# A hybrid decoder layer on one core: longer planned transfers into the row tiles, from the first superblock's end on

## Chip, cores, metric

The kernel runs on one core of one Trainium2 chip. The metric is device microseconds of one execution, as the median of several runs.

## The reference, cut to what matters

One layer of a decoder stack: a norm, one wide projection, three branches (an RWKV-7 recurrence, sliding-window attention with rotary angles and sinks, cross-attention into 256 memory tokens), a gated merge, an output projection and the residual.

```
h = rms_norm(x, norm_g[l])
p = h @ w_in[l]
(p_r, p_k, p_v, p_w, p_a, z_a, p_q, p_sk, p_sv, z_b, p_xq, z_c, p_gate) = jnp.split(p, split_points, axis=-1)
y_a = rwkv7_mix(p_r, p_k, p_v, p_w, p_a, ...) * jax.nn.silu(z_a)
y_b = sliding_window_sink_attn(p_q, p_sk, p_sv, positions, ...) * jax.nn.silu(z_b)
y_c = memory_cross_attn(p_xq, mem, ...) * jax.nn.silu(z_c)
gates = jax.nn.sigmoid(p_gate).reshape(bsz, t, N_BRANCHES, D_MODEL)
merged = (gates[:, :, 0] * (y_a @ w_proj_a[l]) + gates[:, :, 1] * (y_b @ w_proj_b[l])
          + gates[:, :, 2] * (y_c @ w_proj_c[l]))
x = x + merged @ w_out[l]
```

x has 2048 rows of 1024 float32 numbers; w_in is 1024 by 7552.

## The kernel before, in words

**Tiles.** The 2048 tokens are worked in four superblocks of 512. In a superblock, h of the norm lies as eight tiles of 128 channels by 512 tokens, each split into a high part (hH) and a low part (hL) in TensorE's float32r format. A projection (`proj`, `gemm3`, lines 534 to 536) multiplies 8 such tiles by a 128-channel block of w_in: three matmuls for each tile (high by high, low by high, high by low), 24 matmuls of 128x128 by 512, into one of two PSUM banks named mm. The weights are split too: ScalarE copies the high part (L515), VectorE takes the difference (L516). In the first superblock all weights come raw and are split, and most are then kept in DRAM as pairs (k) for the later ones, which load them ready.

**Streams.** Two generators are woven into one program for each superblock: `stream_r` (the recurrence: four prepared pairs of heads, an inversion, a chain of eight chunks) and `stream_f` (cross-attention, sliding window, merges of the branches b and c, and the gates of branch a, each a projection and a tanh, L1306). A third, `x_sums`, loads the next superblock's rows of x for the norm: eight tiles of 128 by 512, all named sx with one buffer, each loaded by ScalarE's queue (L1360) and squared and summed by ScalarE (L1362).

**The end of a superblock.** The merge of branch a (L1321 adds one to the gate and multiplies it with the sum in the mm bank, L1322 adds it to the accumulator mB), the split of the merged tiles (L1326 on ScalarE, L1328 on VectorE) and the output projection (L1338 to L1340, then L1345 adds x, loaded into ya tiles, and L1346 stores) run there. Between them stands the preparation of the next superblock: `rope_tables` loads the positions into an rt tile, computes angles on VectorE (L597 to L616) with two sines on ScalarE (L612, L614); `x_scales` makes the row scales (L1370, L572, L574, L1375); `x_cols` loads eight tiles of x columns into rt tiles by ScalarE's queue (L1384), scales them on VectorE (L1387) and splits them into hH (L1389, ScalarE) and hL (L1390, VectorE). The sine and the tanh of the gates lie in different function tables of ScalarE, and a load of a table (ACT_TABLE_LOAD) stands wherever the order goes from one to the other.

**The planner.** The program order of each engine is not the order of the code. `steps` makes a `Step` of each instruction with its dependences, a rank (its place in the code, moved for some kinds) and costs by the functions `cost_PE`, `cost_ACT` and so on. `lay_out` is a list scheduler: it plays the program forward with these costs, and each engine takes, of the steps that it believes ready at that moment, the one with the lowest rank. `order` then fixes that order on each engine. A DMA costs its queue 420 ns and ends 2200 ns after its issue (4200 for tiles parked in DRAM), not before the wires are free, plus its bytes over 380 a nanosecond. On top comes `late`, which is 5000 for the sx tiles and 0 for all others:

```
if s.bytes:
    wires = s.end = max(wires, s.end) + s.bytes / 380
    s.end += s.late
```

The planner only sets the order. At run time an engine waits in that order for what an instruction really needs. A longer planned transfer makes the steps that read the tile look ready later, so that others are placed ahead of them; and as every later choice depends on the clock of the plan, the order of other engines can move as well.

Of the kernel before, what the change touches and what calls it, by code (L numbers as in the profile page):

```python
# [51 lines left out]

LAT = {"PE": 200, "DVE": 45, "ACT": 35, "POOL": 80, "SP": 30}
NAMES = {mybir.EngineType.PE: "PE", mybir.EngineType.DVE: "DVE", mybir.EngineType.Activation: "ACT",
         mybir.EngineType.Pool: "POOL", mybir.EngineType.SP: "SP"}
# [2 lines left out]
class Step:  # L60


    def __init__(self, ins, masks):
        self.ins, self.eng = ins, NAMES[ins.engine]
        self.reads, self.writes = ([self.region(a.bass_ap, masks) for a in aps if getattr(a, "bass_ap", None) is not None]
                                   for aps in (ins.ins, ins.outs))
        self.reads, self.writes = ([r for r in l if r] for l in (self.reads, self.writes))
        self.before, self.after, self.opens, self.group, self.end, self.next = set(), [], [], [], None, None
        self.lat = LAT[self.eng]
        self.chain = self.eng == "PE" and any(r[0].startswith(("Zt", "W_", "R_")) or r[0] in ("W", "R") for r in self.reads)  # L70
        if self.eng == "PE":
            self.lat = 600
        outs = [a.bass_ap for l in (ins.outs, ins.ins) for a in l if getattr(a, "bass_ap", None) is not None]
        rows = [a.offset // math.prod(list(a.tensor.shape)[1:]) for a in outs[:1] + [a.bass_ap for a in ins.ins if getattr(a, "bass_ap", None) is not None]]
        self.rows = rows[0], max(rows)
        self.bytes = 512 * self.n((self.writes + self.reads)[0]) if self.is_dma() else 0
        getattr(self, "cost_" + ("SP" if self.bytes else self.eng))()

    def is_dma(self):
# [62 lines left out]
    def cost_SP(self):  # L142
        parked = any(r[0].startswith(("fq", "fb", "fv", "fn", "fy")) for r in self.reads + self.writes)
        self.dur, self.busy = 4200 if parked else 2200, 420
        self.late = 5000 if any(r[0].startswith("sx") for r in self.writes) else 0


def steps(instructions, manual, groups, follow, ahead=1000):

    out, masks, seen, byname, opener = [], {}, {}, {}, {}  # L150
    for ins in instructions:
        if isinstance(ins, mybir.BassTilePoolBoundary):
            continue
        s = Step(ins, masks)
        for rs, w in ((s.reads, False), (s.writes, True)):
            for name, parts, words, _, psum, _ in rs:
                s.before |= {q for q, w2, p2, m2 in seen.get(name, ()) if (w or w2 or psum) and q is not s and p2 & parts and m2 & words}
        for name, parts, words, *_ in s.reads:
            seen.setdefault(name, []).append((s, False, parts, words))
        for name, parts, words, *_ in s.writes:  # L160
            old = seen.setdefault(name, [])
            old[:] = [x for x in old if x[0] is s or x[2] & ~parts or x[3] & ~words] + [(s, True, parts, words)]
        s.before |= {byname[x] for x in manual.get(ins.name, ())}
        s.before |= {opener.setdefault(r[0], s) for r in s.writes + s.reads} - {s}
        for b in s.before:
            b.after.append(s)
        byname[ins.name] = s
        s.rank = len(out)
        if any(r[0].startswith(("whl", "raw")) and (s.bytes or r[5] == F32R) for r in s.writes):
            s.rank = max(s.rank - ahead, min(s.rank, FRONT))  # L170
        if s.eng != "PE" and any(r[4] for r in s.reads):
            s.rank -= 600 + 1000 * any(r[0].startswith("mm_") for r in s.reads)
        if s.eng == "DVE" and s.writes and s.writes[0][0].startswith(("ibc", "Yi")):
            s.rank += 500
        out.append(s)
    for a, b in follow.items():
        byname[a].next = byname[b]
    for names in groups:
        group = [byname[n] for n in names]
        group[0].group = group[1:]  # L180
        needs = set().union(*(s.before for s in group)) - set(group)
        for s in group:
            for b in needs - s.before:
                b.after.append(s)
            s.before |= needs
    return out
# [123 lines left out]
def order(tc, manual, groups, follow):  # L310

    orders = lay_out(tc, steps(list(tc.nc.cur_bb.bb.instructions), manual, groups, follow))
    how = mybir.DependencyInfo(mybir.DependencyClass.NoSync, mybir.DependencyReason.DATA)
    for l in orders.values():
        for a, b in zip(l, l[1:]):
            tc.add_manual_dep(b.ins, a.ins.name, how, reason="order")
# [1237 lines left out]
```

## Time and profile before

| | |
|---|---|
| median of three runs | 2141.29 us (2141.21 to 2143.42) |
| the profiled execution | 2142.16 us, its span 2140.3 us |
| TensorE (PE) busy | 2124.0 us |
| its weight loads (PEld) | 1750.1 us |
| VectorE (DVE) | 1429.2 us |
| ScalarE (ACT) | 803.4 us |
| GpSimd (POOL) | 140.5 us |
| granted TensorE clock | 1.000 |

Matmuls are pipelined: a matmul of 512 columns is recorded with 394 ns, and the next one starts earlier than that. In rows of groups the number after the bar is the busy time, then the mean of one in ns, then the idle time of the engine ahead of them. In a timeline row the columns are start, duration, engine (a q behind it is its queue of instructions), line, operation, tiles, and in brackets the idle time of the engine just before and what ended it. In a row of waits stand what waited, at which line, for what, then the total, the number of times and the longest. The superblocks' output projections run at 528 to 572, 1051 to 1095, 1573 to 1616 and 2093 to 2136 us.

### The profile page before, as it was taken

Reading aid. Unit: us, or ns where it says so; the run is one execution under the profiler, and the core shown is the slowest. Engines: PE = TensorE matmul, PEld = TensorE weight load, DVE = VectorE, ACT = ScalarE, POOL = GpSimd, SP = SyncE. Lnnn points to the kernel's source line nnn. Section 1 sums busy time; section 2 is a strip of 40 time slices with the busy share of each in tenths; the row PEclk is TensorE's granted clock in tenths of the full one; section 3 lists DMA queues with packets and bytes.
Section 4 is the critical chain, followed back from the end, with each engine's and each line's share of the span. In section 5 each row is a group of like instructions: output and inputs, shape, how many; then the busy total and the mean of one; then the engine's idle time right before and its main releaser. Section 6 shows DMA issues by size and latency. Waiting matters only on the chain.

```text
span 2140.3 us, 37430 instructions
## 1 busy us (share of the span) xinstructions
PE 2124.0 (99%) x14248; PEld 1750.1 (82%) x14248; DVE 1429.2 (67%) x3246; ACT 803.4 (38%) x1699; POOL 140.5 (7%) x180
## 2 busy tenths in 40 slices
PE   9999999999999999999999999999999999999999
PEld 7888788778888888878788888887888888888787
DVE  7879888568477777546647778736455777873532
ACT  7655555335343343313424434410423334331220
POOL 1001000001001000001001000000100010000000
PEclk9999999999999999999999999999999999999999
DMA  9987898988876678695877667877676666768665
GB/s 333 361 284 266 275 300 273 348 297 263 277 213 200 189 218 233 199 313 189 278 255 216 199 178 229 235 235 256 214 265 215 210 196 203 230 188 273 209 207 180
DMA packets 308594, 519.17 MB, mean 243 GB/s; under 512 B 89280, under 2 KB 175552, under 8 KB 308416
## 3 DMA queue, kind: packets, MB, share of 16 engines
q1 hardware_dynamic: 292288, 487.42, 71.4%
q10 hardware_dynamic: 16128, 29.37, 4.2%
q8 instruction: 113, 1.85, 0.4%
q14 instruction: 65, 0.53, 0.1%
HBM read 378.80 MB, written 137.89 MB: 241 GB/s over the span
## 4 chain that ended last, share of the span: by engine, by line
PE 90%; DVE 4%; DMA 3%; issue 1%; ACT 1%; SPq 0%; POOL 0%; ACTq 0%; DVEq 0%
PE mm L535 22%; PE mm L534 22%; PE mm L536 22%; PE mm L1338 1%; PE mm L1340 1%; PE mm L1339 1%; PE rw L999 1%; PE rw L1016 1%; PE oo L1287 1%; PE rw L831 1%; DVE whl L516 1%; PE rw L850 1%; PE oo L831 1%; DMA raw<-in_w_in 1%; PE rw L921 0%
## 5 line engine op out<-in xcount | busy, mean ns | idle before, releaser
L534 PE MATMUL mm<-hH,whl 128*128 128x512 f32 x1888 | 743.6, 394 | 0.4 <-DVE carry L742 0.4
L535 PE MATMUL mm<-hL,whl 128*128 128x512 f32 x1888 | 743.7, 394 | 0.2 <-DVE hL L1390 0.2
L536 PE MATMUL mm<-hH,whl 128*128 128x512 f32 x1888 | 742.1, 393 | 0.0
L534 PEld LDWEIGHTS mm<-hH,whl 128*128 128x128 f32 x1888 | 354.8, 188 | 71.3 <-ACT big L851 0.7
L535 PEld LDWEIGHTS mm<-hL,whl 128*128 128x128 f32 x1888 | 354.9, 188 | 71.2 <-DVE hL L1390 0.6
L536 PEld LDWEIGHTS mm<-hH,whl 128*128 128x128 f32 x1888 | 354.8, 188 | 70.8
L515 ACT ACTIVATE whl<-raw 128x512 fp32r<-128x512 f32 x174 | 108.9, 628 | 124.8 <-PE mm L536 85.4
L516 DVE TENSOR_TENSOR whl<-raw,whl 128x512 fp32r<-128x512 f32 x174 | 119.9, 691 | 50.2 <-ACT whl L515 48.2
L534 PE MATMUL mm<-yh,whl 128*128 128x512 f32 x384 | 151.0, 393 | 0.1
L535 PE MATMUL mm<-yl,whl 128*128 128x512 f32 x384 | 150.2, 391 | 0.0
L536 PE MATMUL mm<-yh,whl 128*128 128x512 f32 x384 | 150.2, 391 | 0.0
L1306 ACT ACTIVATE gt<-mm 128x512 f32<-128x512 f32 x64 | 38.0, 593 | 216.7 <-PE mm L536 216.5
L534 PEld LDWEIGHTS mm<-yh,whl 128*128 128x128 f32 x384 | 72.1, 188 | 15.7 <-ACT gt L1306 0.5
L535 PEld LDWEIGHTS mm<-yl,whl 128*128 128x128 f32 x384 | 72.1, 188 | 14.9 <-DVE yl L1065 0.3
L536 PEld LDWEIGHTS mm<-yh,whl 128*128 128x128 f32 x384 | 72.1, 188 | 14.8
L1321 DVE SCALAR_TENSOR_TENSOR gt<-gt,mm 128x512 f32<-128x512 f32 x32 | 22.0, 687 | 92.3 <-PE mm L536 92.1
L487 POOL TENSOR_SCALAR st<-st 128x4 f32<-128x4 f32 (+1 forms) x32 | 12.5, 391 | 1004.9 <-DVE st L1219 407.4
L1345 DVE SCALAR_TENSOR_TENSOR ya<-mm,ya 128x512 f32<-128x512 f32 x16 | 11.0, 689 | 94.7 <-PE mm L1340 94.7
L1255 ACT ACTIVATE g<-g,mxs,st 128x128 f32<-128x128 f32 x128 | 61.6, 483 | 26.6 <-DVE mxs L1248 26.6
L892 DVE TENSOR_TENSOR ibc<-km,Yi 128x126 f32<-128x126 f32 (+22 forms) x248 | 62.8, 253 | 6.2 <-DMA km<-fn 0.6
L893 DVE TENSOR_TENSOR Yi<-Yi,ibc 128x126 f32<-128x126 f32 (+22 forms) x248 | 62.9, 254 | 5.5
L491 POOL TENSOR_TENSOR st<-st,mhalf 128x8 f32<-128x8 f32 (+1 forms) x36 | 56.2, 1562 | 3.0
(1807 smaller groups left out, 3586.0 us busy)
## 6 DMA issues: line engine op xcount, KB each, us to landing
whl<-k SPq DMA_DIRECT2D x474, 512.0 KB, 4.1
k<-whl SPq DMA_DIRECT2D x162, 512.0 KB, 4.7
raw<-in_w_in SPq DMA_DIRECT2D x118, 256.0 KB, 4.1
fq<-big SPq DMA_DIRECT2D x64, 256.0 KB, 4.5
fb<-big SPq DMA_DIRECT2D x64, 256.0 KB, 4.7
big<-fq SPq DMA_DIRECT2D x32, 512.0 KB, 6.4
big<-fb SPq DMA_DIRECT2D x32, 512.0 KB, 5.6
ya<-in_x ACTq DMA_DIRECT2D x32, 256.0 KB, 5.5
```

Source lines behind the costliest of these rows:

```text
L491: G.tensor_tensor(out, out, mhalf[:, :n], op=ALU.pow)
L515: S.activation(w[:, 0], raw, AF.Copy)
L516: V.tensor_tensor(w[:, 1], raw, w[:, 0].bitcast(F32), op=ALU.subtract)
L534: PE.matmul(out, lh, rh, start=i == 0, stop=False)
L535: PE.matmul(out, lh, rl, start=False, stop=False)
L536: newest[0] = PE.matmul(out, ll, rh, start=False, stop=i == n - 1).ins.name
L831: m = PE.matmul(g[:, c], BK[h, c0 + c], Q[h, c0 + c], start=True, stop=True)
L892: V.tensor_tensor(bc[:, :m, :w], Nb[:, s, s + 1:].unsqueeze(1).to_broadcast([128, m, w]), B[:, :m, s:s + 1].to_broadcast([128, m, w]), op= ...
L893: V.tensor_tensor(B[:, :m, s + 1:], B[:, :m, s + 1:], bc[:, :m, :w], op=ALU.add)
L1255: S.activation(P_, P_, AF.Exp, scale=r2[:, b, i:i + 1], bias=mx[:, b, i:i + 1], accum_out=mx[:, b, 2 + i:3 + i])
L1306: S.activation(t, gp, AF.Tanh, scale=0.5)
L1321: V.scalar_tensor_tensor(g, g, 1.0, pp, op0=ALU.add, op1=ALU.mult)
```

## The change

`late` is now taken from a small table by the name of the tile that a step writes, and is set to 0 for the first 3000 steps.

```
+LATE = {"sx": 5000, "rt": 3500, "xr": 6000}
...
+        self.late = next((t for n, t in LATE.items() for r in self.writes if r[0].startswith(n)), 0)
...
     def cost_SP(self):
         parked = any(r[0].startswith(("fq", "fb", "fv", "fn", "fy")) for r in self.reads + self.writes)
         self.dur, self.busy = 4200 if parked else 2200, 420
-        self.late = 5000 if any(r[0].startswith("sx") for r in self.writes) else 0
...
         s.rank = len(out)
+        if s.rank < 3000:
+            s.late = 0
```

Only DMAs use `late` in `lay_out`. So loads into rt tiles (the positions and the columns of x at the three boundaries) are planned 3500 ns longer. No DMA writes a tile whose name begins with xr (the rows of x for the output go to ya), so that entry names nothing. The bound of 3000 steps lies inside the first superblock: its first four sx loads come before it and are now planned 5000 ns shorter than before, the other four keep their 5000. The instructions themselves are the same, except for the table loads, which follow from the order.

In the order, TensorE's row differs between about 160 and 500 us of the old trace (the first superblock), and at three small places, one at each boundary. The other engines differ in the same stretches. The changed file is three lines longer, so that each line number there is three higher (L1387 becomes L1390).

VectorE at the second boundary. Before (g2 holds a gate, mm the bank with the projection of branch a, rt the columns of x):

```order
L1322 TENSOR_TENSOR mB_9089<-mB_9089,g2_11070 128x512
L1387 TENSOR_TENSOR rt_11382<-rt_11382,rt_11190 128x512
L1387 TENSOR_TENSOR rt_11387<-rt_11387,rt_11190 128x512
L1321 SCALAR_TENSOR_TENSOR g2_11101<-g2_11101,mm_11335 128x512
L1328 TENSOR_TENSOR mB_11331<-mB_9089,g2_11329 128x512
L516 TENSOR_TENSOR whl_11506<-raw_11507,whl_11506 128x512
L1322 TENSOR_TENSOR mB_9456<-mB_9456,g2_11101 128x512
L1321 SCALAR_TENSOR_TENSOR g2_11132<-g2_11132,mm_11361 128x512
```

And changed:

```order
L1325 TENSOR_TENSOR mB_9089<-mB_9089,g2_11070 128x512
L1331 TENSOR_TENSOR mB_11305<-mB_8938,g2_11303 128x512
L1331 TENSOR_TENSOR mB_11331<-mB_9089,g2_11329 128x512
L1324 SCALAR_TENSOR_TENSOR g2_11101<-g2_11101,mm_11335 128x512
L1325 TENSOR_TENSOR mB_9456<-mB_9456,g2_11101 128x512
L519 TENSOR_TENSOR whl_11506<-raw_11507,whl_11506 128x512
L1331 TENSOR_TENSOR mB_11352<-mB_9456,g2_11350 128x512
L1324 SCALAR_TENSOR_TENSOR g2_11132<-g2_11132,mm_11361 128x512
L1325 TENSOR_TENSOR mB_9556<-mB_9556,g2_11132 128x512
L1331 TENSOR_TENSOR mB_11378<-mB_9556,g2_11376 128x512
L1390 TENSOR_TENSOR rt_11382<-rt_11382,rt_11190 128x512
```

The first two scalings of columns (L1387) stood ahead of the last two products with a gate (L1321); now all products, sums and splits of the merge stand ahead of the first scaling.

ScalarE at the second boundary, some 25 us earlier. Before:

```order
L1306 ACTIVATE g2_11070<-mm_11041 128x512
L612 ACT_TABLE_LOAD
L612 ACTIVATE rt_11160<-rt_11155 128x512
L515 ACTIVATE whl_11260<-raw_11261 128x512
L614 ACTIVATE rt_11160<-rt_11155 128x512
L1362 ACTIVATE sx_11038,ss_6534<-sx_11038 128x512
L1306 ACT_TABLE_LOAD
L1306 ACTIVATE g2_11101<-mm_11072 128x512
L515 ACTIVATE whl_11307<-raw_11308 128x512
L1306 ACTIVATE g2_11132<-mm_11103 128x512
```

And changed:

```order
L1309 ACTIVATE g2_11070<-mm_11041 128x512
L518 ACTIVATE whl_11260<-raw_11261 128x512
L615 ACT_TABLE_LOAD
L615 ACTIVATE rt_11160<-rt_11155 128x512
L1309 ACT_TABLE_LOAD
L1309 ACTIVATE g2_11101<-mm_11072 128x512
L1365 ACTIVATE sx_11038,ss_6534<-sx_11038 128x512
L617 ACT_TABLE_LOAD
L617 ACTIVATE rt_11160<-rt_11155 128x512
L518 ACTIVATE whl_11307<-raw_11308 128x512
L1309 ACT_TABLE_LOAD
L1309 ACTIVATE g2_11132<-mm_11103 128x512
```

The tanh of a gate has come between the two sines, with a load of its table ahead of it and one of the sine's behind. The third boundary has the same pattern.

VectorE in the first superblock, about 263 us into the old trace, where L1275 cuts the probabilities of a head pair to its window (as_ is a PSUM bank with them) and L846 scales the keys of the recurrence. Before:

```order
L839 TENSOR_TENSOR big_2202<-yps_2652,gmask_179 64x512
L516 TENSOR_TENSOR whl_3320<-raw_3321,whl_3320 128x512
L1275 TENSOR_TENSOR g2_3121<-as__3114,over_181 64x256
L1275 TENSOR_TENSOR g2_3133<-as__3126,over_181 64x256
L821 SCALAR_TENSOR_TENSOR rr__2527<-rr__2527,dv_182,rk__2245 128x512
L516 TENSOR_TENSOR whl_3464<-raw_3465,whl_3464 128x512
L846 TENSOR_TENSOR big_2205<-big_2205,Pl_658 128x1024
```

And changed:

```order
L842 TENSOR_TENSOR big_2203<-oo_2653,gmask_179 64x512
L519 TENSOR_TENSOR whl_3320<-raw_3321,whl_3320 128x512
L1278 TENSOR_TENSOR g2_3121<-as__3114,over_181 64x256
L1278 TENSOR_TENSOR g2_3133<-as__3126,over_181 64x256
L1278 TENSOR_TENSOR g2_3121<-as__3114,over_181 64x256
L519 TENSOR_TENSOR whl_3464<-raw_3465,whl_3464 128x512
L1278 TENSOR_TENSOR g2_3133<-as__3126,over_181 64x256
L849 TENSOR_TENSOR big_2205<-big_2205,Pl_658 128x1024
```

All four cuts stand together now (two stood further ahead before), L821 and the first shift of the next keys (L740) have moved ahead of them, and L846 follows the last cut directly. On TensorE, 38 large matmuls instead of 24 stand between the products of the recurrence (L831) and the ones that need the cuts (L1287). On ScalarE in the same superblock the Square of the second sx tile stands ahead of L1170 and three rows behind its load, where it stood behind L1172 and six rows behind.

More of the change, by code (lines that the diff above doesn't have):

```diff
@@ L51 @@
 NPV = _n
+LATE = {"sx": 5000, "rt": 3500, "xr": 6000}
 LAT = {"PE": 200, "DVE": 45, "ACT": 35, "POOL": 80, "SP": 30}
@@ L76, in __init__ @@
         self.bytes = 512 * self.n((self.writes + self.reads)[0]) if self.is_dma() else 0
+        self.late = next((t for n, t in LATE.items() for r in self.writes if r[0].startswith(n)), 0)
         getattr(self, "cost_" + ("SP" if self.bytes else self.eng))()
@@ L144, in cost_SP @@
         self.dur, self.busy = 4200 if parked else 2200, 420
-        self.late = 5000 if any(r[0].startswith("sx") for r in self.writes) else 0
 def steps(instructions, manual, groups, follow, ahead=1000):
@@ L168, in steps @@
         s.rank = len(out)
+        if s.rank < 3000:
+            s.late = 0
         if any(r[0].startswith(("whl", "raw")) and (s.bytes or r[5] == F32R) for r in s.writes):
```

## The prediction

> **What bounds the kernel now.** I read the page first (busy shares, chain), then the waits of TensorE by stretch, then the timelines where they lie.
>
> ```profile
> PE 2124.0 (99%) x14248; PEld 1750.1 (82%) x14248; DVE 1429.2 (67%) x3246; ACT 803.4 (38%) x1699; POOL 140.5 (7%) x180
> PE 90%; DVE 4%; DMA 3%; issue 1%; ACT 1%; SPq 0%; POOL 0%; ACTq 0%; DVEq 0%
> ```
>
> TensorE is busy 99% of the span, and 90% of the chain that ended last is its own matmuls. The change takes no matmul away and only moves instructions, so it can win no more than the pauses of TensorE, and lose only what new pauses cost. The pauses lie in few places. Three stretches are touched by the new order: the first superblock (140 to 500 us), and the second and third boundary between superblocks (around 1050 and 1570 us); the first boundary (520 to 580 us) too. The waits of TensorE in the first superblock (what it waited for; us in total, times, longest):
>
> ```profile
> PE oo L1287 <- DVE g L1275: 1.0, 1, 1.0
> PE rw L850 <- DVE big L846: 1.0, 1, 1.0
> PE rw L831 <- DVE big L820: 0.8, 1, 0.8
> PE rw L1008 <- DMA big<-fb: 0.5, 1, 0.5
> PE mm L534 <- DVE carry L742: 0.4, 1, 0.4
> PE rw L1008 <- DVE W L1001: 0.2, 1, 0.2
> ```
>
> And from 1000 to 1100 us:
>
> ```profile
> PE mm L1338 <- issue: 1.3, 1, 1.3
> PE mm L1338 <- DVE g L1321: 0.5, 1, 0.5
> ```
>
> That is 3.9 us in the first superblock and 1.8 us at the second boundary, together 5.7 us: the whole stock that this change can draw on. At the other two boundaries the same view has next to nothing, and I leave them at nothing.
>
> **The second boundary: -1.8 us.** The timeline of VectorE there:
>
> ```profile
> 1045.85 0.69 DVE L1387 TENSOR_TENSOR rt<-rt 128x512 f32<-128x512 f32 x1
> 1049.16 0.69 DVE L1387 TENSOR_TENSOR rt<-rt 128x512 f32<-128x512 f32 x1 [2.63 <-DMA rt<-in_xt]
> 1049.77 0.68 DVE L1321 SCALAR_TENSOR_TENSOR g<-g,mm 128x512 f32<-128x512 f32 x1
> 1055.91 0.68 DVE L1328 TENSOR_TENSOR mB<-mB,g 128x512 fp32r<-128x512 f32 x1
> ```
>
> TensorE's, in which L536 is the last matmul ahead of the output projection (L1338):
>
> ```profile
> 1048.89 0.39 PE L536 MATMUL mm<-yh,whl 128*128 128x512 f32 x1
> 1050.56 0.47 PE L1338 MATMUL mm<-whl,g 128*128 128x512 f32 x1 [1.28 <-issue]
> 1052.91 0.50 PE L1338 MATMUL mm<-whl,g 128*128 128x512 f32 x1 [0.50 <-DVE g L1321]
> ```
>
> The first three loads of x columns on ScalarE's queue:
>
> ```profile
> 1041.56 2.37 ACTq L1384 DMA_DIRECT2D rt<-in_xt  x3
> ```
>
> And the time from issue to landing of all 24:
>
> ```profile
> DMA to landing us min/median/max: 3.3/5.5/8.2
> ```
>
> VectorE stands 2.63 us on the second column tile. Behind it is L1321, which reads an mm bank that the output projection wants: L1321 ends at 1049.77 + 0.68 = 1050.45, and TensorE starts 0.11 us later. The same lateness makes the second pause. The planner took 2.2 us and the bytes (262144 / 380 = 0.69 us) for a load that takes 5.5; the changed one takes 3.5 more, 6.4. In the new order both L1321 and everything else that TensorE waits for stand ahead of the first L1387, as the rows of VectorE in the section on the change show. The L1328 that will stand just ahead of it starts at 1055.91 today, so about 1053 without the 2.63; a load issued from 1041.56 on, or even 5 us later (on ScalarE the issues move behind two L1326), has its 5.5 us by then. I take both pauses as gone, 1.28 + 0.50 = 1.8 us. Were a load to take the longest 8.2 us, the wait would sit behind the last L1328, where only a weight split (L516) follows it.
>
> What comes later for that: the tiles of the next superblock's h. At the first boundary the last two now stand behind the first four output sums. VectorE there, today:
>
> ```profile
> 547.05 1.63 DVE L1390 SCALAR_TENSOR_TENSOR hL<-rt,c_pv,hH 128x512 fp32r<-128x512 f32 x2
> 551.00 0.68 DVE L1345 SCALAR_TENSOR_TENSOR ya<-as__6168,ya 128x512 f32<-128x512 f32 x1
> 569.94 0.69 DVE L1345 SCALAR_TENSOR_TENSOR ya<-mm,ya 128x512 f32<-128x512 f32 x1 [15.66 <-PE mm L1340]
> ```
>
> Today h is done at 548.7; in the new order about 554, two L1387 and two L1390 after 551.7. TensorE works on the output until 569.9, so some 15 us cover it; without that cover the 5 us would show.
>
> **Table loads: +0.** At the second and third boundary a tanh of a gate (L1306) now stands between the two sines (L612, L614), so ScalarE switches tables four times at each instead of twice: four loads more in all. ScalarE at the second boundary today:
>
> ```profile
> 1016.80 1.28 ACT L612 ACT_TABLE_LOAD   x1
> 1018.09 0.63 ACT L612 ACTIVATE rt<-rt 128x512 f32<-128x512 f32 x1
> 1021.98 0.60 ACT L1306 ACTIVATE g<-mm 128x512 f32<-128x512 f32 x1
> 1027.06 0.60 ACT L1306 ACTIVATE g<-mm 128x512 f32<-128x512 f32 x1 [2.09 <-PE mm L536]
> ```
>
> 4 x 1.28 = 5.1 us of ScalarE. Between the gates at 1021.98 and 1027.06 there will be the gate 0.60, two loads 2.56, a sine 0.63, a weight split 0.63 and the Square of sx 0.62 (both below): 5.04 us in 5.08. The later gate comes at most a little late, and its bank is wanted one projection (24 matmuls, 5.4 us) later. So it costs nothing; with no cover at all it costs 5.1.
> The Trainium skill, "ScalarE: Activation LUTs", sections "What ACT_TABLE_LOAD costs" and "Table sets: the hidden batching unit", speaks against this change: finish one set before switching, since each switch takes about 1.28 us and a drain of about 1.38 us. By that, an estimate, the four switches would take 10.6 us of ScalarE. The trace has the 1.28 but not the drain: the sine starts 0.01 us after its load.
>
> **The first superblock: -1.0 us, from -3.9 to +3.9.** Four loads of x rows (sx) are planned 5 us shorter there, and everything behind is laid out anew. The two longest pauses on TensorE:
>
> ```profile
> 262.59 0.39 PE L535 MATMUL mm<-hL,whl 128*128 128x512 f32 x1
> 262.81 0.39 PE L536 MATMUL mm<-hH,whl 128*128 128x512 f32 x1
> 264.20 0.29 PE L1287 MATMUL oo<-g,Vt 64*64 64x128 f32 x1 [1.00 <-DVE g L1275]
> 266.63 1.09 PE L850 MATMUL rw<-c_ident,big 128*128 128x128 f32 x8 [0.98 <-DVE big L846]
> ```
>
> VectorE around them:
>
> ```profile
> 263.63 0.42 DVE L1275 TENSOR_TENSOR g<-as__3126,over 64x256 f32<-64x256 f32 x1
> 264.08 0.75 DVE L821 SCALAR_TENSOR_TENSOR rr__2527<-rr__2527,dv,rk__2245 128x512 f32<-128x512 f32 x1
> 264.75 0.68 DVE L516 TENSOR_TENSOR whl<-raw,whl 128x512 fp32r<-128x512 f32 x1
> 265.35 1.22 DVE L846 TENSOR_TENSOR big<-big,Pl 128x1024 f32<-128x1024 f32 x1
> 266.60 0.75 DVE L740 SCALAR_TENSOR_TENSOR rk__3041<-mm,c_pv,rk__3041 128x511 f32<-128x511 f32 x1
> ```
>
> In the new order 38 large matmuls instead of 24 stand between L831 and this L1287: 14 x 0.227 = 3.2 us more cover (two matmuls start 0.22 to 0.23 us apart). VectorE gets L821, L740, a tiny copy and one L516 ahead of L1275: 0.75 + 0.75 + 0.1 + 0.68, about 2.2 us by their starts. Cover grows by 1.0, the size of the pause. And L846 now follows the last L1275 directly: 1.22 us against the 1.4 us that L1287's block keeps TensorE. So this place should give about 2.0. Two other things are unknown. The other four pauses (1.9 us) may move, and the new order may have pauses of its own, which no row of before can show. I bound them by the stretch's present total: 3.9 us again, or none. Between 1.9 (the four stay, nothing new) and 3.9 (as many as now) I take the middle, 2.9: a gain of 1.0. The range goes from all gone (-3.9) to twice as many (+3.9).
>
> **Sum.** -1.8 + 0 - 1.0 = -2.8 us. The profiled execution took 2142.16 us (span 2140.3), so 2139.4; the median of the three runs is 2141.29, 0.87 lower, so the forecast there is 2138.5.
>
> **The rivals.**
> *More is won in the first superblock (faster).* The new layout leaves no pause: -1.8 - 3.9 = -5.7, 2135.6. For it: the two largest pauses, half of the 3.9, have visible cover now. Against: VectorE is the crowded engine there, and four pauses are not aimed at.
> *Nothing is won.* The 1.8 comes back as new pauses in the first superblock: 2141.3. The trace cannot exclude it.
> The Trainium skill, "DMA: Bandwidth & Descriptors", section "Anatomy of one DMA", puts a transfer at about 2.0 us plus bytes over 436 GB/s, an estimate of 2.6 us for these. By that rule the old plan was right, and longer planned times only push work back, with no gain: this same case. The rows say 5.5 at the median and at least 3.3, so I give that rule little.
> *Slower: ScalarE stands on sx.* Its Square is now planned 5 us earlier in the first superblock, before the data is there. The Square, in all 24 cases:
>
> ```profile
> L1362 ACT ACTIVATE sx<-sx x24: 614/622/643, 116.4 to 1557.9; 128x512 f32<-128x512 f32 x24
> ```
>
> Its loads, from issue to landing:
>
> ```profile
> DMA to landing us min/median/max: 2.6/4.6/6.2
> ```
>
> ScalarE around the second of these loads:
>
> ```profile
> 150.33 0.35 ACTq L1360 DMA_DIRECT2D sx<-in_x  x1
> 154.79 0.63 ACT L515 ACTIVATE whl<-raw 128x512 fp32r<-128x512 f32 x1 [0.93 <-PE mm L536]
> 157.51 0.60 ACT L1170 ACTIVATE g<-mm 128x512 f32<-128x512 f32 x1 [2.09 <-PE mm L536]
> ```
>
> Planned with 2.2, landing in 4.6 (6.2 at the longest), four times: 9.6 to 16 us of ScalarE, with gates and weight splits queued behind. From a level of -2.8, over 7.1 us of the 16 must reach TensorE to be slower by 0.2%; all of it would give 2152. Against: at the second load the Square goes ahead of L1170, behind the split that ends at 155.4, and the data is there at 154.9, at the longest 156.5; L1170 can't start before 157.5 anyway.
>
> **How the numbers follow.** 0.2% is 4.3 us, about what a measurement of this kernel can tell from no change. Chances: the forecast 0.50, nothing won 0.21, the full 5.7 won (or nearly) 0.19, slower through sx or several new pauses 0.10. Only the third is faster by over 4.3 us, only the fourth slower by that: 0.19, 0.71, 0.10. The range runs from all pauses gone, 2135.6, to twice the pauses in the first superblock, -1.8 + 3.9 = +2.1, 2143.4.
>
> **What would show it.** Right: no wait of TensorE by L1338 around 1050 us and no VectorE wait on in_xt ahead of L1321; four table loads more, and no TensorE wait that names them; TensorE's waits from 140 to 500 us add up to about 2.9 instead of 3.9. Wrong: a wait on ScalarE for sx with a TensorE wait behind it, waits in the first superblock over 6 us or under 1.5, or a time that moves with matmuls closer or wider than 0.227 us apart, which no term here foresees.

## The result, and the profile after

The changed kernel takes 2136.57 us (median of 18 runs, 2135.41 to 2140.74), the kernel before 2141.97 us in the runs beside it (18 too, 2139.31 to 2148.31). The ratio is 0.9976 with a 95% interval of 0.9969 to 0.9982, so 5.1 us less, from 3.9 to 6.6. That is faster by a little over 0.2%. The forecast was 2138.5, 2.8 us less than the median: its sign and its range hold, its size is about half of what was measured, and the interval leaves the 2.8 out.

The profiled execution of the changed kernel took 2139.91 us, which is one of its longer ones. Its page, busy shares and then the shares of the chain that ended last:

```profile
PE 2123.9 (99%) x14248; PEld 1751.5 (82%) x14248; DVE 1430.2 (67%) x3246; ACT 808.2 (38%) x1703; POOL 140.5 (7%) x180
PE 92%; DVE 3%; DMA 3%; ACT 1%; issue 1%; POOL 0%; SPq 0%; ACTq 0%; DVEq 0%
```

TensorE does the same work in the same time (2123.9 after, 2124.0 before). ScalarE has four instructions more and 4.8 us more busy time: the four table loads. TensorE's part of the chain goes from 90% to 92%, VectorE's from 4% to 3%.

The waits of TensorE from 140 to 500 us:

```profile
PE rw L1011 <- DMA big<-fb: 2.2, 1, 2.2
PE rw L834 <- DVE big L823: 0.6, 1, 0.6
PE as__3431 L1239 <- DVE g L1212: 0.3, 1, 0.3
PE as__4106 L1272 <- DVE g L1268: 0.3, 1, 0.3
PE rw L1011 <- DVE W L1004: 0.2, 1, 0.2
```

The two longest of before, at L1287 and L850 (now L1290 and L853), are gone; two of 0.3 us at L1239 and L1272 are new. The 2.2 us on big<-fb, a tile that comes back from DRAM, were 0.5 us in the profile of before. The same view from 1000 to 1100 us has no row at all any more, where 1.3 and 0.5 us stood, and from 500 to 580 us none either, where 0.3 us stood.

TensorE at the place of the two pauses (no bracket: no wait ahead of it):

```profile
267.24 0.30 PE L1290 MATMUL oo<-g,Vt 64*64 64x128 f32 x1
268.62 1.09 PE L853 MATMUL rw<-c_ident,big 128*128 128x128 f32 x8
```

VectorE there:

```profile
266.67 0.43 DVE L1278 TENSOR_TENSOR g<-as__3126,over 64x256 f32<-64x256 f32 x1
267.13 1.23 DVE L849 TENSOR_TENSOR big<-big,Pl 128x1024 f32<-128x1024 f32 x1
```

L849 follows the last cut (L1278) directly and ends at 268.36, before TensorE reaches L853 at 268.62.

VectorE at the second boundary:

```profile
1050.38 0.68 DVE L1324 SCALAR_TENSOR_TENSOR g<-g,mm 128x512 f32<-128x512 f32 x1
1052.49 0.69 DVE L1331 TENSOR_TENSOR mB<-mB,g 128x512 fp32r<-128x512 f32 x1 [0.70 <-ACT g L1329]
1053.10 0.68 DVE L1390 TENSOR_TENSOR rt<-rt 128x512 f32<-128x512 f32 x1
```

And TensorE:

```profile
1049.94 0.39 PE L539 MATMUL mm<-yh,whl 128*128 128x512 f32 x1
1050.17 0.39 PE L1341 MATMUL mm<-whl,g 128*128 128x512 f32 x1
```

The last product with a gate (L1324) stands ahead of the first column tile, and the column tile starts behind the last L1331 with no wait for its load. The first output matmul follows L539 after 0.23 us, the usual distance of two matmuls. Before, it followed the last L536 after 1050.56 - 1048.89 = 1.67 us, so TensorE lost 1.44 us there, and the view of waits shows 1.28 of it. The view counts from the end of the matmul ahead as it is recorded, 0.39 us after its start, although without a pause the next one starts after 0.23. A pause is therefore longer than its wait by some 0.16 us, and one of less than that doesn't show in the view at all. The section on the prediction reads the starts for that reason.

ScalarE at the second boundary, the two sines (L615, L617) with the gate between them:

```profile
1020.61 1.28 ACT L615 ACT_TABLE_LOAD   x1
1021.90 0.63 ACT L615 ACTIVATE rt<-rt 128x512 f32<-128x512 f32 x1
1022.55 1.28 ACT L1309 ACT_TABLE_LOAD   x1
1023.85 0.60 ACT L1309 ACTIVATE g<-mm 128x512 f32<-128x512 f32 x1
...
1027.54 1.28 ACT L1309 ACT_TABLE_LOAD   x1
1028.83 0.60 ACT L1309 ACTIVATE g<-mm 128x512 f32<-128x512 f32 x1
```

Each instruction starts 0.01 to 0.02 us behind its table load, and no wait of TensorE names one of these gates.

### The profile page after: what moved, and what is told of

The parts are those of the page before. It is cut to its first block, busy times and chain, and to the rows that moved or that the text cites. A ratio compares the mean times of both kernels' runs of the same rounds, so it can differ in the third digit from the quotient of the medians.

```text
span 2138.0 us, 37423 instructions
## 1 busy us (share of the span) xinstructions
PE 2123.9 (99%) x14248; PEld 1751.5 (82%) x14248; DVE 1430.2 (67%) x3246; ACT 808.2 (38%) x1703; POOL 140.5 (7%) x180
## 4 chain that ended last, share of the span: by engine, by line
PE 92%; DVE 3%; DMA 3%; ACT 1%; issue 1%; POOL 0%; SPq 0%; ACTq 0%; DVEq 0%
PE mm L537 23%; PE mm L538 23%; PE mm L539 23%; PE mm L1343 1%; PE mm L1341 1%; PE mm L1342 1%; PE oo L1290 1%; PE rw L1019 1%; PE rw L1002 1%; PE rw L834 1%; PE rw L853 1%; DVE whl L519 1%; PE oo L834 1%; DMA raw<-in_w_in 1%; PE rw L916 0%
## 5 line engine op out<-in xcount | busy, mean ns | idle before, releaser
L539 PE MATMUL mm<-hH,whl 128*128 128x512 f32 x1888 | 742.6, 393 | 0.0
L539 PEld LDWEIGHTS mm<-hH,whl 128*128 128x128 f32 x1888 | 354.8, 188 | 71.0
L539 PE MATMUL mm<-yh,whl 128*128 128x512 f32 x384 | 150.6, 392 | 0.0
L539 PEld LDWEIGHTS mm<-yh,whl 128*128 128x128 f32 x384 | 72.3, 188 | 15.0
L1324 DVE SCALAR_TENSOR_TENSOR gt<-gt,mm 128x512 f32<-128x512 f32 x32 | 22.0, 687 | 93.1 <-PE mm L539 93.0
```

Source lines behind the costliest of these rows:

```text
L539: newest[0] = PE.matmul(out, ll, rh, start=False, stop=i == n - 1).ins.name
L1324: V.scalar_tensor_tensor(g, g, 1.0, pp, op0=ALU.add, op1=ALU.mult)
```

## The experiments

Two theories were tested. **Pauses by late reads:** an engine is made to stand on a tile before its data is there, and the longer planned transfers take the standing away at the boundaries (the rt part), while the new layout takes the place at 263 us away (the sx part). **The rivals:** the gain comes from the table loads or the angles, or from a layout that is better by chance wherever it is disturbed, or only from one of the two parts. In the expectations theory A is the first of these. Theory B puts all of the gain down to the new layout of the first superblock. Theory C has the pause at the second boundary mostly longer than the 1.8 us of the one profile. All edits are of the changed kernel unless the text says otherwise.

### One part at a time

Only the rt tiles are planned longer, and the sx tiles keep their 5 us everywhere:

```
-        if s.rank < 3000:
+        if s.rank < 3000 and s.late != 5000:
```

> Only the loads into rt tiles are planned longer; all sx loads keep their 5000 as before, so the first superblock has its old order. Theory A (the gain has two parts, the pause at the second boundary and the pauses around 263 us of the first superblock): 1.8 to 2.5 us under the kernel before, 0.9988 to 0.9992, no TensorE wait by the output projection around 1050 us, and the old waits at L1290 and L853 (1.0 us each) still there. Theory B (all of the gain is the new layout of the first superblock): within 0.5 us of the kernel before. Theory C (the boundary pause differs from execution to execution and is mostly longer than the 1.8 us of the one profile): 4 to 5 us under the kernel before, 0.998.

Measured: ratio 0.9985 (0.9977 to 0.9994), so 3.2 us less (1.3 to 4.9). That leaves out theory B; it is more than theory A's 1.8 to 2.5 us and less than theory C's 4 to 5, but the interval reaches both. The waits of TensorE from 140 to 500 us begin as before the change:

```profile
PE oo L1290 <- DVE g L1278: 1.0, 1, 1.0
PE rw L853 <- DVE big L849: 1.0, 1, 1.0
PE rw L834 <- DVE big L823: 0.8, 1, 0.8
```

There is no row from 500 to 580 or from 1000 to 1100 us.

Only the sx tiles are changed:

```
-LATE = {"sx": 5000, "rt": 3500, "xr": 6000}
+LATE = {"sx": 5000, "xr": 6000}
```

> Only the first four sx loads are planned 5 us shorter; rt loads as before, so the boundaries have their old order. Theory A: 2.5 to 3.3 us under the kernel before (0.9985 to 0.9988), the waits at L1290 and L853 gone, the two waits of the output projection around 1050 us (1.3 and 0.5) back. Theory B: 5 us under, 0.9976, the same as the full change. Theory C: within 1 us of the kernel before.

Measured: ratio 0.9986 (0.9977 to 0.9995), 3.0 us less (1.1 to 4.9). That is in theory A's range; the interval leaves out, though barely, the 5 us of theory B and the at most 1 us of theory C. In the first superblock the two pauses are gone. The waits from 1000 to 1100 us:

```profile
PE mm L1341 <- DVE g L1324: 0.5, 1, 0.5
PE mm L1341 <- issue: 0.3, 1, 0.3
```

The pauses at the second boundary are back, and at the first the 0.2 us ahead of L577. So each part does its own work in its own place, and each alone is measurably faster than before. Set against the full 5.1 us, rt is worth between 5.1 - 3.0 = 2.1 and 3.2 us, sx between 5.1 - 3.2 = 1.9 and 3.0 us. These are middle values; each comparison leaves up to 1.9 us to either side.

### Without the four table loads

The positions are planned short as before, the columns of x long, so that the tanh doesn't come between the sines:

```
-        if s.rank < 3000:
+        if s.rank < 3000 or s.late == 3500 and s.eng == "SP":
```

> The full change, but the loads of the positions are planned short as before, so the two sines stand together again: nine table loads instead of thirteen. The loads of x columns stay long, though one scaling of columns now stands ahead of the last product with a gate. Theory A and C: the same time as the full change within 0.7 us, since the four extra table loads (5.1 us of ScalarE) wait behind matmuls. A rival (the four loads reach TensorE): 2.5 to 5 us under the full change.

Measured: ratio 0.9981 (0.9972 to 0.9990), 4.1 us less (2.1 to 6.0): not to be told from the full change. Taking the four loads away gains nothing that can be measured, and the 2.5 to 5 us on top of the 5.1 that they would give if they reached TensorE lie outside the interval. So they are hidden. Its waits have none from 1000 to 1100 us, but the 0.3 us ahead of L577 are there (VectorE reads the positions early again), while the output projection at the first boundary takes 43.33 us from the start of its first L1341 to the start of its last L1343, about as in after (43.29). With the columns planned short it takes 43.62 (the sx part alone). That parts the two small gains at the first boundary: one belongs to the positions, the other to the columns.

### The opposite sign

The rt tiles are planned 1.5 us shorter than before the change, the sx tiles as before it:

```
-LATE = {"sx": 5000, "rt": 3500, "xr": 6000}
+LATE = {"sx": 5000, "rt": -1500, "xr": 6000}
...
-        if s.rank < 3000:
+        if s.rank < 3000 and s.late != 5000:
```

> The other way: rt loads are planned 1500 ns shorter than before, sx as before, so two scalings of columns at the second boundary stand one product with a gate earlier each than in the kernel before. Theory A and C: VectorE stands longer on the loads of columns there, and TensorE pauses 2 to 5 us at the second boundary instead of 1.8: 0.5 to 3 us slower than before, 1.0002 to 1.0014. Theory B: within 0.5 us of before.

Measured: ratio 1.0018 (1.0009 to 1.0027), 3.9 us more than before (1.9 to 5.8), more than the 0.5 to 3 us that I expected, since I had counted the second boundary alone. The waits of TensorE from 1000 to 1100 us:

```profile
PE mm L537 <- DVE g L1324: 1.8, 1, 1.8
PE mm L1341 <- DVE g L1324: 0.3, 1, 0.3
```

And VectorE in that stretch:

```profile
1051.04 0.69 DVE L1390 TENSOR_TENSOR rt<-rt 128x512 f32<-128x512 f32 x1 [3.48 <-DMA rt<-in_xt]
1051.65 0.68 DVE L1324 SCALAR_TENSOR_TENSOR g<-g,mm 128x512 f32<-128x512 f32 x1
```

VectorE stands 3.48 us on a column tile, and the L1324 behind it frees a bank that TensorE wants. At the first boundary it stands 3.8 us on the positions in one piece:

```profile
DVE rt L600 <- DMA rt<-in_positions: 3.8, 1, 3.8
```

There TensorE now waits 0.8 and 0.5 us, and at the third boundary, where the output projection waited for nothing before, it waits 0.4 us for a product with a gate. From start to start of the same matmuls, the three boundaries take 1.5, 1.4 and 0.7 us longer than in the mean of the four profiles of before, about 3.5 us together. So the time follows the planned length of the rt transfers in both directions, by the waits that the theory names. A layout that is only better by chance when disturbed would have no reason to do that.

### The same kernels profiled again

Since the waits on loads differ from one execution to the next, the two kernels were profiled again: before three more times, after two more times. Two of the runs of before and one of after are a single profiled execution each:

> The kernel before, profiled once more. Theory A: the waits at L1287 and L850 around 263 us are 1.0 us each again (they follow from the order alone), and the two waits of the output projection around 1050 us together are 1.8 us again. Theory C: those at 1050 us differ from profile to profile, from 0.8 to 4 us, since they hang on a transfer.

> The kernel before, profiled a third time, with the same expectations: equal waits at 263 us in all profiles; at 1050 us equal waits by theory A, 0.8 to 4 us by theory C.

> The full change, profiled once more. Theories A and C: no TensorE wait at L1290, L853 or the output projection around 1050 us in this profile either; the 2.2 us wait on a parked tile (big from fb) in the first superblock and the 1.2 us later start were of that execution and are smaller here, so that the span is 2134 to 2136 us.

The other two were timed as well:

> The kernel before against itself, so that the accuracy of a comparison is seen: a ratio of 1.0000 within 0.0010. In the profile the waits at L1287 and L850 are 1.0 us each for the fourth time, and the wait of the output projection around 1050 us lies between 0 and 2 us.

> The full change timed once more: 0.9970 to 0.9982. In the profile no TensorE wait at L1290, L853, at the table loads or at the output projection around 1050 us.

Before against itself gave 1.0006 (0.9996 to 1.0015), which shows that such a comparison is good to about 0.1%, 2 us. After gave 0.9979 (0.9970 to 0.9988), 4.5 us less (2.6 to 6.4), as in the first comparison.

The pauses at the second boundary with the order of before were 1.8 us in the first profile, then 1.4, 0.0 and 1.4. The one with none, VectorE at the second boundary:

```profile
1045.46 1.34 DVE L1387 TENSOR_TENSOR rt<-rt 128x512 f32<-128x512 f32 x2 [0.17 <-DMA rt<-in_xt]
```

There the column tile came 0.17 us late where it had been 2.63 us late in the first profile. So this pause does differ from execution to execution, as theory C has it, but the other waits there are shorter than the first profile's, not longer. In all three profiles of after there is no wait at the first two boundaries. At 263 us the pauses of 1.0 and 1.0 us stand in all four profiles of before and in none of after. The waits of TensorE from 140 to 500 us in the second profile of after:

```profile
PE rw L1019 <- DVE Zt L1017: 1.2, 1, 1.2
PE rw L834 <- DVE big L823: 0.5, 1, 0.5
PE as__4106 L1272 <- DVE g L1268: 0.5, 1, 0.5
PE as__3431 L1239 <- DVE g L1212: 0.3, 1, 0.3
PE rw L1011 <- DVE W L1004: 0.2, 1, 0.2
```

In the third they are 0.8, 0.8, 0.4, 0.3 and 0.2. So the sums over this stretch are 3.9, 5.2, 4.4 and 3.6 us before (mean 4.3) and 3.6, 2.7 and 2.5 us after (mean 2.9).

### The wait for big<-fb

The loads of big tiles that come back from DRAM (from fb, and from fq too) are planned 2 us longer as well:

```
-LATE = {"sx": 5000, "rt": 3500, "xr": 6000}
+LATE = {"sx": 5000, "rt": 3500, "big": 2000, "xr": 6000}
```

> The full change, and the loads of parked tiles into big tiles planned 2000 ns longer as well (from step 3000 on). Theory A: the wait at L1011 on big from fb (0.5 to 2.2 us in the first superblock) goes, 0.5 to 2 us under the full change, 0.9966 to 0.9974 of before. Rival: the chain that reads these tiles is laid later and pauses elsewhere: the same as the full change or up to 3 us slower.

Measured: ratio 0.9973 (0.9961 to 0.9984), 5.8 us less than before (3.4 to 8.4), not to be told from the change itself. The wait for big<-fb is not in its profile, but waits of 0.6, 0.6, 0.4, 0.3 and 0.2 us are. It shows no better version.

### Which of the four sx loads

Only the first two loads are planned shorter (and rt as before the change):

```
-LATE = {"sx": 5000, "rt": 3500, "xr": 6000}
+LATE = {"sx": 5000, "xr": 6000}
...
-        if s.rank < 3000:
+        if s.rank < 1900:
```

> Only the first two sx loads are planned 5 us shorter (the bound is 1900 instead of 3000), rt as before. TensorE's order is that of the run with the four sx loads alone, row for row. Theory A: the same time as that run, 0.9981 to 0.9990, and the waits at L1290 and L853 gone. Rival (the gain hangs on the early sums of squares of all four loads): half of it, 0.9992 or more.

Measured: ratio 0.9994 (0.9985 to 1.0003), 1.3 us less (3.2 less to 0.6 more). I missed that: TensorE's order is that of the sx part alone and its two pauses are gone, and yet the gain is not clear of zero. The interval overlaps that of the sx part (0.9977 to 0.9995), so it doesn't show either that the other two loads matter. Its profile has the gain: the stretch of TensorE from 225 to 361 us, whose order is new, takes 135.0 us there, as in the three profiles of after (134.8 to 135.5) and not as in the four of before (136.9 to 137.0).

Only the other two, with the bound the other way:

```
-LATE = {"sx": 5000, "rt": 3500, "xr": 6000}
+LATE = {"sx": 5000, "xr": 6000}
...
-        if s.rank < 3000:
+        if 1900 < s.rank < 3000:
```

> Only the third and fourth sx loads are planned 5 us shorter, rt as before. TensorE's order is that of the kernel before, row for row; on ScalarE the Square of the third load stands three rows behind its load instead of seven. Theory A: the time of the kernel before, 0.9993 to 1.0007, with both waits of 1.0 us around 263 us. Rival (ScalarE standing on sx costs time): ScalarE waits 1 to 2.5 us for sx and the run is 1 to 3 us slower.

Measured: ratio 0.9998 (0.9989 to 1.0007), nothing, as expected. The waits of TensorE from 140 to 500 us have the two pauses again:

```profile
PE rw L1011 <- DMA big<-fb: 1.9, 1, 1.9
PE oo L1290 <- DVE g L1278: 1.0, 1, 1.0
PE rw L853 <- DVE big L849: 1.0, 1, 1.0
```

So the layout that covers the place at 263 us comes from the first two loads.

## Why the prediction was right or wrong

**The second boundary, -1.8: the mechanism right, the size right by luck.** VectorE no longer stands on a column tile ahead of the product that frees a bank, and the pauses are gone wherever the columns are planned long (six profiles of six: three of after, the rt part alone, the one without the table loads, the one with big). With the columns planned as before, seven profiles have waits of 1.8, 1.4, 0.0, 1.4, 0.8, 1.0 and 1.7 us, a mean of 1.2, and the 1.8 was the highest of them, as the wait hangs on when a load lands. But the waits are not the whole loss. An output projection without a pause takes 43.29 us from its first start to its last, in the fourth superblock of every profile. What it took over that, with the distance ahead of its first matmul less the usual 0.23 us, is 2.4, 1.9, 0.0, 2.0, 1.4, 1.6 and 2.3 us in the same seven, a mean of 1.7, and 0.0 in the six. So two errors cancel in the 1.8: the longest wait was taken for the usual one, and a view that leaves out part of each pause was taken for the loss.

**"At the other two boundaries the same view has next to nothing, and I leave them at nothing": wrong by about 0.8 us at the first.** TensorE there, before:

```profile
519.88 0.66 PE L574 MATMUL as__5914<-c_ident,rt 128*128 128x128 f32 x4 [0.28 <-DVE rt L572]
...
550.17 0.39 PE L1340 MATMUL mm<-whl,mB 128*128 128x512 f32 x1
550.54 0.50 PE L1338 MATMUL as__6330<-whl,g 128*128 128x512 f32 x1
```

And after:

```profile
521.60 0.60 PE L577 MATMUL as__5914<-c_ident,rt 128*128 128x128 f32 x4
```

VectorE waits before, from 480 to 560 us:

```profile
DVE rt L597 <- DMA rt<-in_positions: 1.4, 1, 1.4
```

VectorE stood on the positions and came late with the scales (L572), and the view has 0.2 to 0.3 us of TensorE in every profile with the positions planned as before. From the start of the matmul ahead of L574 to the start of the one behind its four matmuls, it is 1.0 to 1.1 us before and 0.6 after, so 0.5. The output projection of the first superblock, from the start of its first L1338 to the start of its last L1340, took 43.61 to 43.67 us in the four profiles of before and 43.29 in the three of after. The row at 550.54 lies in that stretch: it starts 0.37 us behind the one ahead of it instead of 0.23, and the view of waits names nothing there, as the matmul ahead is recorded up to 550.56. Both pieces are small but stand in every execution. I read the view of waits alone and passed over a 0.3.

**Table loads, +0: right.** The four loads are there, and the version without them is no faster. Between the gates at 1023.85 and 1028.83 ScalarE's row is as full as I had worked out, and no TensorE wait names them. The Trainium skill's drain ("ScalarE: Activation LUTs", "What ACT_TABLE_LOAD costs") doesn't show in the rows: 1.28 us of a load, and the gate starts 0.01 to 0.02 us after.

**The first superblock, -1.0: the place right, the size too small.** The place at 263 us gives its 2.0 us of waits in every profile of the new order. What I took back for new pauses, 1.0, was the middle of two bounds and no reading. That the 2.9 us left standing are also the mean of the three profiles after (2.9) is luck: of these, 0.9 us on average is big<-fb, a wait that comes and goes by execution (0.5, 1.4, 0.8 and 0 before; 2.2, 0 and 0.4 after) and is no effect of the change. I also set them against the 3.9 of one profile, where the mean of four is 4.3, so that the waits of the whole superblock give 1.4 us. Nearer to the change is the stretch in which TensorE's order is new, the 950 matmuls from 224.68 to 361.67 us of the first profile. It takes 137.0 us as the mean of the seven profiles with the old order and 134.7 as that of the seven with the new one (134.8, 134.9 and 135.5 in after itself), so the term measures 2.3 us.

**The sum.** By the waits of all profiles it is -1.2 - 0.3 + 0 - 1.4 = -2.9 us, near the forecast and under the measurement. By the starts it is -1.7 - 0.8 + 0 - 2.3 = -4.8 us (-4.4 with the three profiles of after alone in the last term), which lies in the measured 3.9 to 6.6. So the mechanism and the places were right, and what was too small is the stock of 5.7 us and the terms drawn from it: the waits of one profile's view, with nothing for the first boundary and 1.0 us taken back for new pauses.

The profiled spans differ by less: the mean of four before is 2139.1 us (2140.3, 2140.7, 2136.4, 2139.1), of three after 2136.1 (2138.0, 2134.6, 2135.8), 3.0 us less. The stretch around big<-fb, from 407 to 439 us, accounts for 0.9 us of what is missing. It took 31.8 to 33.2 us in the four of before and 32.6 and 32.2 in two of after, but 35.1 in the first profile of after. That one has the 2.2 us of wait there and then 3.4 us with a granted clock of 0.5. The first 133 us account for another 0.3. Whether the last two of the four sx loads bring anything stays open.

**The rivals.** More won in the first superblock, down to no pause: no, about 2.9 us of waits still stand there. That the time comes near to that rival's 2135.6 has another reason, the first boundary and the part of each pause that the view leaves out. Nothing won: no, both parts gain by themselves. With it falls the rule drawn from the Trainium skill's "DMA: Bandwidth & Descriptors" ("Anatomy of one DMA"), by which the old plan was long enough. The section gives its figure for transfers that GpSimd issues, and these loads are issued by ScalarE. With rt planned 3.5 us longer the kernel is faster, with 1.5 us shorter slower, and the 24 column loads land in 5.9 us at the median after the change. Their row:

```profile
DMA to landing us min/median/max: 2.9/5.9/7.7
```

Slower through ScalarE on sx: no. ScalarE waits once for a load of sx ahead of its Square, 0.3 us, and in the three profiles of after no wait of TensorE in that stretch names the Square. (The 2152 that the prediction gives for this rival doesn't follow from its numbers: all 16 us on top of 2138.5 would be 2154.5.)

## What to carry to other kernels

A planner that fixes the order should be given the time that a load takes in the running kernel, from issue to landing (here 5.5 us at the median, where 2.9 were planned): what stands on a late tile on an in-order engine also holds up the unrelated step behind it that frees a bank. Price the places of such waits from more than one execution, since a wait on a DMA is a draw, while one that followed from the order of the engines (the place at 263 us) was the same each time. Price them from start to start of the same matmuls, with and without the pause, and not by the idle time that a view shows: here the view gave 2.9 us and the starts 4.8, where 3.9 to 6.6 were measured. And count the small waits that stand in every execution, as a 0.3 at each of several places is worth as much as one of the long ones.

## What the hardware showed that was not expected

The same wait on a load differs widely from execution to execution of the same order: 0.0 to 1.8 us of TensorE at the second boundary, 0 to 1.4 us (before) and 0 to 2.2 us (after) for big<-fb. The waits at L1287 and L850 repeat to 0.1 us (1.0 and 1.0, four times of four). Not every wait between engines does: L1272 on VectorE's L1268 was 0.3, 0.5 and 0.8 us in the three profiles of after. Profiles of one kernel differ by up to 4.3 us in their spans, nearly what this change is worth, while the kernel before, timed against itself, came out at 1.0006.

In the two profiles with the longest wait for big<-fb, 2.2 us (the first of after, and the one with the rt tiles planned shorter), the granted clock was 0.5 for 3.4 us shortly behind it, from about 416 to 420 us. The same matmuls around it took 35.1 and 35.0 us there, against 33.2 us in the profile with a wait of 1.9 and the full clock. No run shows whether the wait brought the lower clock on.
